# Three pairs of projection units of the second layer as seven half-size products each, with weight sums made by accumulating transfers

## The chip, the cores and the metric

The kernel runs on one core of a Trainium2 chip. Its time is the device time of one execution in microseconds (us); the kernel before takes 886.24 us, the median of three runs that lie between 886.05 and 886.3. The five engines are TensorE (PE, with its weight loads listed as PEld), VectorE (DVE), ScalarE (ACT), GpSimd (POOL) and SyncE (SP). Each works through its own list of instructions in order. SP issues nearly all loads; POOL issues a few.

## The reference

A trunk of two layers on 256 tokens of width 2048, all in float32. What matters here is the second layer's input projection `z = h @ w_in`:

```python
def odd_layer(x, norm, w_in, w_alpha, b_alpha, head_norm, v_norm, w_s, b_s, w_out):
    h = rms_norm(x, norm)
    z = h @ w_in                                  # (256, 2048) @ (2048, 6160)
    q, k, v, a_lr, gc, u, vd, gd = jnp.split(z, split_points(ODD_SIZES), axis=-1)
    log_a = jax.nn.log_sigmoid((a_lr @ w_alpha + b_alpha)) / GLA_TAU
    ...
    o = gla_chunked(heads(q, GLA_DK), heads(k, GLA_DK), heads(v, GLA_DV), heads(log_a, GLA_DK))
    yc = rms_norm(o, head_norm).reshape(bsz, seq, GLA_VW) * jax.nn.silu(gc)
    yd = spatial_gating(jax.nn.gelu(u), jax.nn.gelu(vd), w_s, b_s, v_norm) * jax.nn.silu(gd)
    return jnp.concatenate([yc, yd], axis=-1) @ w_out
```

The column widths are q 512, k 512, v 1024, a_lr 16, gc 1024, u 1024, vd 1024, gd 1024.

## The kernel before

Activations stand transposed in SBUF, 16 row blocks (k = 0 to 15) of 128, each with a high part and a low part of the 256 tokens: a float32 number is split into a value rounded to the type fp32r and the rest, so that a product of two float32 matrices is three fp32r products (high by high, high by low, low by high). `act2` is the tile that holds the second layer's activations so.

Weights come in **units**. A unit of 512 columns is four transfers of 1 MB, each a tile `raw` of 128 x 2048 that holds four row blocks. `halves` (L114) loads them through SP into a pool of three buffers and makes two half tiles of 128 x 1024 of each: ACT rounds it to `whi` (L123, "cast"), DVE subtracts to `wlo` (L73, "sub"). Both pools have four buffers, so casts run at most four half tiles ahead of the matmuls that read them. `by_token` (L135) then has `products` (L127) multiply: per row block and per token block b of 128 tokens three matmuls of 512 columns (L131 to L133). A half tile of a 512-column unit feeds 12 matmuls, a unit 96. The result is two PSUM banks, one per token block.

Smaller work (decays, attention-like parts, gates, transposes) is written as Python generators that are spawned after a unit and advanced by `tick` inside later units; a scheduler then fixes the order of each engine's list when the program is built, and picks buffers from the pools.

The second layer's units, by their first transfer in `w_in1`: a unit of 272 columns (v and a_lr, from `w_va`), 0 (256 columns of v), 2 (v), 6 (q), 10 (k), 14 and 18 (vd), 22 and 26 (gc), 30 and 34 (u), 38 and 42 (gd). `onward` (L492) ends the first layer: it transposes the residual and writes the last parts of `act2`.

Of the kernel before, what the change touches and what calls it, by code (L numbers as in the profile page):

```python
# [51 lines left out]
def trunk(ctx, tc, x, xt, lead, w_in0, w_out0, w_va, w_in1, w_out1, w_gate, small, dist, cst, w_alpha, w_s,  # L52
          r_balpha, r_hnorm, r_vnorm, r_fnorm, out):
    nc = tc.nc

    def pool(name, bufs, **kw):
        return ctx.enter_context(tc.tile_pool(name=name, bufs=bufs, **kw))

    one = pool("one", 1)
    actp = pool("actp", 2)  # L60
    rawp = pool("rawp", 3)
    hip = pool("hip", 4)
    lop = pool("lop", 4)
# [71 lines left out]
    def by_token(w, unit, act, n=512, order=None, before=None, during=None, ps=None):  # L135


        at = 0 if ps is None else LEAD
        ps = ps or [psm.tile([P, n], F32, name="ps", tag="ps") for _ in range(2)]
        order = order or list(range(KT))  # L140
        deep = 1024 // n if n != NVA else 4
        skip = at // (2 * deep)
        for hi, lo in halves(w, unit + skip, KT // (2 * deep) - skip, 2 * deep * n):
            if before is not None:
                for k in order[at:at + deep]:
                    before(k)
            for kk in range(deep):
                products(ps, act, order[at], hi[:, kk * n:(kk + 1) * n], lo[:, kk * n:(kk + 1) * n],
                         at == 0, at == KT - 1)
                if during is not None:  # L150
                    during(at, hi)
                at += 1
                tick(max(n // 256, 1))
        return ps

    def by_channel(w, unit, act):

        ps = [psm.tile([P, 2, T], F32, name="pc", tag="ps") for _ in range(2)]
        k = 0
        for hi, lo in halves(w, unit, 2):  # L160
            for kk in range(4):
                for c in range(2):
                    at = kk * 256 + c * P
                    wh, wl = hi[:, at:at + P], lo[:, at:at + P]
                    if k:
                        nc.tensor.matmul(ps[c][:, 1, :], wl, act[:, k, 0:T], start=False, stop=False)  # L166
                    nc.tensor.matmul(ps[c], wh, act[:, k, :], start=(k == 0), stop=(k == KT - 1))  # L167
                    if k == 0:
# [27 lines left out]
    sm = one.tile([P, S_ALL], F32, name="sm")  # L196
    cs = one.tile([P, C_ALL], F32, name="cs")
    xs = one.tile([P, 2, D], F32, name="xs")
    warm = one.tile([P, P], F32, name="warm")
    nc.vector.memset(warm, 0.0)  # L200
    table = tiny.tile([P, 1], F32, name="table", tag="table", bufs=1)
    nc.scalar.copy(table, warm[:, 0:1])
# [21 lines left out]
    for k in range(LEAD):  # L224
        raw = rawp.tile([P, T + 1024], F32, name="first", tag="raw")
# [4 lines left out]
        part = raw[:, 0:T]  # L230
# [294 lines left out]
    def decay(alr):  # L525
# [27 lines left out]
        for b in range(2):  # L553
# [13 lines left out]
            nc.scalar.activation(dec[:, :, 2 * b:2 * b + 2], dp[:, :, :, 0], AF.Exp)  # L567
            yield 3

    v1 = [big_tile([P, 2, 512], f"vv{c}") for c in range(2)]  # L570
    ps = by_token(w_va, 0, act2, n=NVA)
    alr = tiny.tile([P, 2, 16], F32, name="alr", tag="alr", bufs=1)
    for b in range(2):
# [8 lines left out]
        nc.scalar.activation(v1[1][:, b, :], ps[b], AF.Copy, scale=rs1[:, b:b + 1])  # L582
    drain()
    eb, enb, ebl = decays
    ps = by_token(w_in1, 6, act2)
    for b in range(2):
        nc.vector.scalar_tensor_tensor(out=eb[:, b, :], in0=ps[b], scalar=rs1q[:, b:b + 1], in1=eb[:, b, :],
                                       op0=ALU.mult, op1=ALU.mult)
    ps = by_token(w_in1, 10, act2)
    for b in range(2):  # L590
        for t in (enb, ebl):
            nc.vector.scalar_tensor_tensor(out=t[:, b, :], in0=ps[b], scalar=rs1[:, b:b + 1], in1=t[:, b, :],
                                           op0=ALU.mult, op1=ALU.mult)
    qt, kt, kd = eb, enb, ebl
    osb = []
# [61 lines left out]
        gla_ro.append(rsqrt_of(sso.rearrange("p a b -> p (a b)"), 8, T, "ro"))  # L657

    spawn(gla())


    wst = mid_tile([P, 4, P], "wst")
# [3 lines left out]
                            base=0, channel_multiplier=-1)  # L666
    vf = []
    mv = tiny.tile([P, 8, 2], F32, name="mv", tag="mv", bufs=1)
    for c in range(2):
        ps = by_token(w_in1, 14 + 4 * c, act2)  # L670
        t = big_tile([P, 2, 512], f"vf{c}")
        for b in range(2):
            nc.scalar.activation(t[:, b, :], ps[b], AF.Gelu_apprx_tanh, scale=rs1[:, b:b + 1])
            for i in range(2):
                bs = tiny.tile([P, 6], F32, name="bs", tag="bs", bufs=2)
                nc.vector.bn_stats(bs, t[:, b, i * T:(i + 1) * T])
                nc.vector.bn_aggr(mv[:, c * 4 + b * 2 + i, :], bs)
        vf.append(t)
# [5 lines left out]
    hn = big_tile([P, 2, 512], "hn")  # L684
    nc.gpsimd.dma_start(out=hn, in_=r_hnorm.partition_broadcast(P))

    yt1 = actp.tile([P, KT, 2 * T], F32R, name="yt1", tag="act")

    def transposed(src, k0, b):
        tp = psa.tile([P, 4, P], F32, name="tp", tag="a")  # L690
        for i in range(4):
            nc.tensor.transpose(tp[:, i, :], src[:, i * P:(i + 1) * P], ident)
        split(yt1, slice(k0, k0 + 4), b * P, P, tp)

    def gla_gate(c, ps):
        for b in range(2):
            sg = sp_tile([P, 512], "sgc")
            nc.scalar.activation(sg, ps[b], AF.Silu, scale=rs1[:, b:b + 1])
            nc.vector.tensor_mul(sg, sg, hn[:, c, :])
            for i in range(2):  # L700
                o = osb[b][:, c, i * T:(i + 1) * T]
                at = b * 4 + 2 * c + i
                nc.vector.scalar_tensor_tensor(out=o, in0=o, scalar=ro[:, at:at + 1], in1=sg[:, i * T:(i + 1) * T],
                                               op0=ALU.mult, op1=ALU.mult)
        for b in range(2):
            yield 4
            transposed(osb[b][:, c, :], 4 * c, b)

    def normed(c):
        for b in range(2):  # L710
            for i in range(2):
                t = vf[c][:, b, i * T:(i + 1) * T]
                at = c * 4 + b * 2 + i
                nc.vector.tensor_scalar(out=t, in0=t, scalar1=mv[:, at, 0:1], scalar2=rv[:, at:at + 1],
                                        op0=ALU.subtract, op1=ALU.mult)
            nc.vector.tensor_mul(vf[c][:, b, :], vf[c][:, b, :], vn[:, c, :])
            yield 6

    yd = []
# [189 lines left out]
```

## Time and profile before

| what | value |
|---|---|
| median of three runs | 886.24 us |
| the profiled execution | 885.52 us |
| its span | 883.4 us |
| PE busy | 873.2 us (99% of the span) |
| DVE busy | 530.6 us (60%) |
| ACT busy | 480.7 us (54%) |
| POOL busy | 13.2 us (1%) |
| DMA | 163.42 MB, mean 185 GB/s |
| granted TensorE clock | 0.998 |

The profiled execution took 885.52 us, of which 883.4 are the span from its first to its last recorded work; 2.1 us lie around it. It is 0.7 us under the median of the runs. A busy PE is not a PE at its peak, since matmuls overlap and their ends are modelled; the time of a stage is better read from the distance between starts. [...]

### The profile page before, as it was taken

How to read it: one execution, taken by the hardware profiler on the slowest of the kernel's cores; microseconds unless marked ns; L12 is line 12 of the kernel's file. 1: busy time of each engine (PE TensorE's matmuls, PEld its weight loads, DVE VectorE, ACT ScalarE, POOL GpSimd, SP SyncE). 2: the span in 40 equal slices, each digit the busy share in tenths (PEclk: the TensorE clock that was granted, in tenths of full speed). 3: DMA queues.
4: the chain of work that ended last, by engine and by line, in shares of the span. 5: the costliest groups of instructions: out<-in, count | busy, mean ns of one | idle time of the engine just before them, and what ended most of it. 6: DMA issues, size and time to landing. Idle time of an engine off the chain costs nothing.

```text
span 883.4 us, 11332 instructions
## 1 busy us (share of the span) xinstructions
PE 873.2 (99%) x4480; PEld 733.8 (83%) x4480; DVE 530.6 (60%) x770; ACT 480.7 (54%) x709; POOL 13.2 (1%) x27
## 2 busy tenths in 40 slices
PE   8999999999999999999999999999999999999996
PEld 7878888888888888888888988886688888888886
DVE  7596457667677576666555744564267554555562
ACT  5775556676676766554444564333555444544452
POOL 0100000000000000010000000000000000000000
PEclk9999999999999999999999999999999999999999
DMA  8875554454444435555455544552365544555532
GB/s 288 351 266 191 191 202 157 152 192 161 176 178 167 167 144 191 189 208 191 181 178 186 185 151 183 191 191 95 105 253 214 190 158 177 191 191 190 191 143 96
DMA packets 25492, 163.42 MB, mean 185 GB/s; under 512 B 2896, under 2 KB 3408, under 8 KB 7008
## 3 DMA queue, kind: packets, MB, share of 16 engines
q1 hardware_dynamic: 24048, 158.41, 49.9%
q0 software_dynamic: 1248, 4.23, 1.4%
q8 instruction: 35, 0.57, 0.3%
q14 instruction: 17, 0.14, 0.0%
q10 hardware_dynamic: 144, 0.07, 0.0%
HBM read 160.60 MB, written 2.10 MB: 184 GB/s over the span
## 4 chain that ended last, share of the span: by engine, by line
PE 94%; DVE 2%; DMA 1%; ACT 1%; issue 1%; POOL 0%; ACTq 0%
PE pc L167 20%; PE ps L131 18%; PE ps L132 18%; PE ps L133 18%; PE pc L166 10%; DVE wlo L73 1%; PE up L626 1%; DMA xs<-in_x 1%; PE pc L169 1%; PE sc L352 1%; PE gp L436 1%; PE gp L435 1%; ACT whi L123 1%; DVE act L212 0%; PE pt_ps L370 0%
## 5 line engine op out<-in xcount | busy, mean ns | idle before, releaser
L73 DVE TENSOR_TENSOR wlo<-raw,whi 128x1024 fp32r<-128x1024 f32 x280 | 341.7, 1223 | 259.0 <-ACT whi L123 258.8
L123 ACT CAST whi<-raw 128x1024 fp32r<-128x1024 f32 x280 | 293.7, 1052 | 306.2 <-PE ps L133 224.1
L167 PE MATMUL pc<-act,whi 128*128 128x512 f32 x768 | 269.7, 394 | 0.0
L131 PE MATMUL ps<-whi,act 128*128 128x512 f32 (+2 forms) x544 | 208.8, 386 | 0.8 <-DVE la_s L325 0.8
L166 PE MATMUL pc<-act,wlo 128*128 128x256 f32 x720 | 208.4, 289 | 0.0
L132 PE MATMUL ps<-wlo,act 128*128 128x512 f32 (+2 forms) x544 | 205.8, 379 | 1.0 <-DVE wlo L73 0.9
L133 PE MATMUL ps<-whi,act 128*128 128x512 f32 (+2 forms) x544 | 205.5, 378 | 0.0
L167 PEld LDWEIGHTS pc<-act,whi 128*128 128x128 f32 x768 | 142.6, 188 | 29.4
L166 PEld LDWEIGHTS pc<-act,wlo 128*128 128x128 f32 x720 | 135.8, 189 | 2.5 <-DVE wlo L73 0.8
L131 PEld LDWEIGHTS ps<-whi,act 128*128 128x128 f32 x544 | 102.1, 188 | 25.2 <-issue 6.5
L132 PEld LDWEIGHTS ps<-wlo,act 128*128 128x128 f32 x544 | 102.3, 188 | 20.2 <-DVE wlo L73 2.5
L133 PEld LDWEIGHTS ps<-whi,act 128*128 128x128 f32 x544 | 102.2, 188 | 19.0
L131 PE MATMUL ps<-whi,yt 128*128 128x512 f32 (+1 forms) x256 | 97.0, 379 | 0.0
L133 PE MATMUL ps<-whi,yt 128*128 128x512 f32 (+1 forms) x256 | 96.3, 376 | 0.0
L132 PE MATMUL ps<-wlo,yt 128*128 128x512 f32 (+1 forms) x256 | 96.2, 376 | 0.0
L133 PEld LDWEIGHTS ps<-whi,yt 128*128 128x128 f32 x256 | 48.2, 188 | 8.9
L132 PEld LDWEIGHTS ps<-wlo,yt 128*128 128x128 f32 x256 | 48.2, 188 | 8.6
L131 PEld LDWEIGHTS ps<-whi,yt 128*128 128x128 f32 x256 | 48.2, 188 | 8.4
L188 ACT ACTIVATE junk<-xs 128x512 f32<-128x512 f32 (+1 forms) x26 | 15.3, 591 | 15.7 <-DVE xs L771 14.3
L175 ACT COPY z<-pc 128x256 f32<-128x256 f32 x24 | 8.7, 372 | 13.0 <-PE pc L167 13.0
L175 ACT COPY qk<-pc 128x256 f32<-128x256 f32 x24 | 8.7, 372 | 12.1 <-PE pc L167 12.1
L428 DVE SCALAR_TENSOR_TENSOR xc<-z,sm,xc 128x255 f32<-128x255 f32 (+2 forms) x36 | 14.7, 475 | 0.0
(231 smaller groups left out, 621.5 us busy)
## 6 DMA issues: line engine op xcount, KB each, us to landing
raw<-in_w_in SPq DMA_DIRECT2D x108, 1024.0 KB, 4.8
raw<-in_w_out SPq DMA_DIRECT2D x32, 1024.0 KB, 4.8
raw<-in_w_va SPq DMA_DIRECT2D x2, 1088.0 KB, 5.0
xs<-in_x SPq DMA_DIRECT2D x2, 1024.0 KB, 6.0
out<-xs SPq DMA_DIRECT2D x8, 256.0 KB, 2.7
first<-in_lead SPq DMA_DIRECT2D x3, 640.0 KB, 6.1
xt<-in_xt SPq DMA_DIRECT2D x6, 256.0 KB, 7.5
wg<-in_w_gate POOLq DMA_DIRECT2D x6, 256.0 KB, 5.1
```

The lines of the kernel that those rows point to most:

```text
L73: nc.vector.tensor_tensor(out=o, in0=a, in1=hi.bitcast(F32), op=ALU.subtract)
L123: nc.scalar.copy(hi, raw[:, cols])
L131: nc.tensor.matmul(ps[b], xh, wh, start=first, stop=False)
L132: nc.tensor.matmul(ps[b], xh, wl, start=False, stop=False)
L133: nc.tensor.matmul(ps[b], xl, wh, start=False, stop=last)
L166: nc.tensor.matmul(ps[c][:, 1, :], wl, act[:, k, 0:T], start=False, stop=False)
L167: nc.tensor.matmul(ps[c], wh, act[:, k, :], start=(k == 0), stop=(k == KT - 1))
L169: nc.tensor.matmul(ps[c][:, 1, :], wl, act[:, k, 0:T], start=False, stop=False)
L175: nc.scalar.copy(dst, ps[:, 1, :])
L188: nc.scalar.activation(junk[:, :src.shape[-1]], src, AF.Square, accum_out=acc)
L352: nc.tensor.matmul(sc[:, 1:3, :], qk[:, 0, P:T], qk[:, 1, :], start=True, stop=True)
L428: nc.vector.scalar_tensor_tensor(out=xch[:, t:], in0=z[:, :T - t], scalar=cw[3 - t], in1=xch[:, t:], op0=ALU.mult, op1=ALU.add)
```

## The change

Two units that share the activations, A and B, are taken together as a pair. The activations are cut into four blocks (two halves of the 2048 rows by two token blocks), the weights into four (two halves of the rows by two units), and the 2 x 2 product is made by Strassen's scheme in Winograd's form: seven half-size products of 8 row blocks, one token block and 512 columns. One such product ("run") is 24 matmuls, a pair 168 instead of 192. Pairs are (6, 10), (14, 18) and (30, 34).

Three things are new. The **forms**, four sums of activation blocks, are made by DVE and split by ACT and DVE into a second tile `sums2` of the size of `act2`. The **weight sums** are made in place: a `raw` tile is loaded by SP, cast and multiplied, and then POOL issues a transfer that adds another 1 MB of weights onto what stands in it; one pair of tiles (x0) is loaded once and added to three times, another (y0) is added to once, a third (z0) only loaded. That is six plain transfers and eight adding ones of 1 MB in a pair, where two units had eight plain ones. The **combination** of the products takes two ACT copies and five DVE operations of 128 x 512. A half tile now feeds 6 matmuls, so that a pair has 28 casts and 28 subs where two units had 16 of each.

The pool of `raw` tiles grows from three to five buffers; `warm` and `rb` move into the pool of `sg`; the reserve that GpSimd's transfers use shrinks (`dynamic_dma_scratch_size=1024`). The gate units 22 and 26 move: 22 now stands between the first and the second pair, 26 between the second and the third, and their results wait in `sgc` tiles. `yt1` is made after the third pair.

```diff
-    rawp = pool("rawp", 3)
+    rawp = pool("rawp", 5)
...
+    def pair(w, ua, ub, act, forms):
+        f3, f5, f6, f7 = forms
+        x0, y0, z0 = ([rawp.tile([P, 2048], F32, name="raw", tag="raw") for _ in range(2)] for _ in range(3))
+        def load(raws, u):
+            for i, raw in enumerate(raws):
+                nc.sync.dma_start(out=raw, in_=w[u + i])
+        def add(raws, u):
+            for i, raw in enumerate(raws):
+                nc.gpsimd.dma_start(out=raw, in_=w[u + i], accum_op=ALU.add)
+        def run(ps, a, raws, first, last):
+            tile_, k0, b = a
+            for i, raw in enumerate(raws):
+                for s in range(2):
+                    cols = slice(s * 1024, (s + 1) * 1024)
+                    hi = hip.tile([P, 1024], F32R, name="whi", tag="whi")
+                    lo = lop.tile([P, 1024], F32R, name="wlo", tag="wlo")
+                    nc.scalar.copy(hi, raw[:, cols])
+                    sub(lo, raw[:, cols], hi)
+                    for kk in range(2):
...
+                        nc.tensor.matmul(ps, xh, wh, start=(first and j == 0), stop=False, skip_group_check=not first)
+                        nc.tensor.matmul(ps, xh, wl, start=False, stop=False, skip_group_check=not first)
+                        nc.tensor.matmul(ps, xl, wh, start=False, stop=(j == 7), skip_group_check=not first)
+                        tick(1)
...
+        load(x0, ua)
+        load(y0, ub + 2)
+        m12, m3, m56, m7 = bank(), bank(), bank(), bank()
+        run(m12, (act, 0, 0), x0, True, False)
+        s1 = mid_tile([P, 512], "s1")
+        nc.scalar.copy(s1, m12)
+        add(x0, ub)
+        run(m3, f3, y0, True, True)
+        add(y0, ub)
+        run(m56, f5, x0, True, False)
+        s5 = mid_tile([P, 512], "s5")
+        nc.scalar.copy(s5, m56)
+        add(x0, ub + 2)
+        run(m7, f7, y0, True, True)
+        load(z0, ua + 2)
+        run(m56, f6, x0, False, True)
+        add(x0, ua + 2)
...
+        run(m12, (act, 8, 0), z0, False, True)
+        m4 = bank()
+        run(m4, (act, 8, 1), x0, True, True)
+        nc.vector.tensor_tensor(out=s5, in0=m4, in1=s5, op=ALU.add)
+        return [m12, s5], [t, c22]
...
+    sums2 = actp.tile([P, KT, 2 * T], F32R, name="sums2", tag="act")
+    def make_forms():
+        for i in range(2):
...
+            s, r = (sp_tile([P, 4, P], n) for n in ("fs", "fr"))
+            minus(s, part(0, 1), part(8, 1))
+            minus(r, part(0, 1, T), part(8, 1, T))
+            plus(s, s, r)
+            keep(1, s)
+            yield 3
...
+    spawn(make_forms())
     ps = by_token(w_va, 0, act2, n=NVA)
...
-    ps = by_token(w_in1, 6, act2)
+    ps, ps_k = pair(w_in1, 6, 10, act2, forms2)
...
-    ps = by_token(w_in1, 10, act2)
...
+    keep_gate(0)
...
-    for c in range(2):
-        ps = by_token(w_in1, 14 + 4 * c, act2)
+    for c, ps in enumerate(pair(w_in1, 14, 18, act2, forms2)):
...
+    keep_gate(1)
...
-    for c in range(2):
-        ps = by_token(w_in1, 30 + 4 * c, act2)
+    for c, ps in enumerate(pair(w_in1, 30, 34, act2, forms2)):
...
-    nc = bacc.Bacc("TRN2", target_bir_lowering=False, num_devices=1)
+    nc = bacc.Bacc("TRN2", target_bir_lowering=False, num_devices=1, dynamic_dma_scratch_size=1024)
```

How the lists of instructions change is shown at three places. In their rows a name before the arrow is the tile written, names behind it the tiles read, numbers at a name tell buffers' tiles apart.

First POOL, from the last transfer of the first layer's end (`bal`) on. Before, it goes on with small transfers (`wst`, `vn`, `hn`) and a memset:

```order
L486 DMA bal_3682<-in_r_balpha 128x512
L663 DMA wst_5070<-in_w_s 128x512
L665 ISA
L665 AFFINE_SELECT wst_5070<-wst_5070 128x512
L603 MEMSET att_5096 128x1024
L683 DMA vn_5518<-in_r_vnorm 128x1024
L685 DMA hn_5520<-in_r_hnorm 128x1024
```

Now the eight adding transfers of the first pair stand there (4833 and 4834 are x0, 4835 and 4836 are y0):

```order
L555 DMA bal_3682<-in_r_balpha 128x512
L172 DMA raw_4833<-in_w_in1 128x2048
L712 MEMSET att_5176 128x1024
L172 DMA raw_4834<-in_w_in1 128x2048
L172 DMA raw_4835<-in_w_in1 128x2048
L172 DMA raw_4836<-in_w_in1 128x2048
L172 DMA raw_4833<-in_w_in1 128x2048
L172 DMA raw_4834<-in_w_in1 128x2048
L172 DMA raw_4833<-in_w_in1 128x2048
L172 DMA raw_4834<-in_w_in1 128x2048
L781 DMA wst_5362<-in_w_s 128x512
```

Each of the tiles x0 is named three times in that list, and each naming has to wait for the casts of the one before; the other two pairs have the same eight rows.

Second DVE, from the last sub of the 272-column unit to the second sub of unit 0. Before, little stands between them beside the last two parts of `act2`:

```order
L73 TENSOR_TENSOR wlo_4443<-raw_4412,whi_4442 128x1088
L507 TENSOR_TENSOR xg_4359<-tp_4354,sm_91 128x512
L73 TENSOR_TENSOR act2_3857<-xg_4359,act2_3857 128x4x128
L507 TENSOR_TENSOR xg_4380<-tp_4375,sm_91 128x512
L73 TENSOR_TENSOR act2_3857<-xg_4380,act2_3857 128x4x128
L73 TENSOR_TENSOR wlo_4480<-raw_4477,whi_4479 128x1024
L73 TENSOR_TENSOR wlo_4531<-raw_4477,whi_4530 128x1024
```

Now the operations on the forms (`fs`, `fr`, written by L649, and `sums2`) stand there:

```order
L73 TENSOR_TENSOR wlo_4514<-raw_4511,whi_4513 128x1024
...
L73 TENSOR_TENSOR sums2_4332<-fs_4335,sums2_4332 128x4x128
L73 TENSOR_TENSOR act2_3857<-xg_4367,act2_3857 128x4x128
L649 TENSOR_TENSOR fr_4336<-fr_4336,act2_3857 128x512
L73 TENSOR_TENSOR act2_3857<-xg_4392,act2_3857 128x4x128
L649 TENSOR_TENSOR fs_4335<-act2_3857,fr_4336 128x512
L73 TENSOR_TENSOR sums2_4332<-fr_4336,sums2_4332 128x4x128
L649 TENSOR_TENSOR fs_4335<-fs_4335,act2_3857 128x512
...
L73 TENSOR_TENSOR sums2_4332<-fs_4465,sums2_4332 128x4x128
L73 TENSOR_TENSOR wlo_4569<-raw_4511,whi_4568 128x1024
```

Of the 28 form operations 20 stand between the last sub of the 272-column unit and the second sub of unit 0 (`wlo_4569`), and 26 ahead of its third (`wlo_4606`).

Third SP, behind the loads of the 272-column unit. Before, one run of plain loads; now the six loads of each pair (L168) stand between the loads of the other units (L118):

```order
L118 DMA raw<-in_w_in 128x2048 x46
```

```order
L118 DMA raw<-in_w_in 128x2048 x6
L168 DMA raw<-in_w_in 128x2048 x6
L118 DMA raw<-in_w_in 128x2048 x4
L168 DMA raw<-in_w_in 128x2048 x6
L118 DMA raw<-in_w_in 128x2048 x4
L168 DMA raw<-in_w_in 128x2048 x6
L118 DMA raw<-in_w_in 128x2048 x8
```

SP issues 40 instead of 46 loads there; the 24 adding transfers are POOL's.

## Rows read from the trace of the kernel before

**Rows 1.** The page: busy time by engine, and the chain of waits

```profile
PE 873.2 (99%) x4480; PEld 733.8 (83%) x4480; DVE 530.6 (60%) x770; ACT 480.7 (54%) x709; POOL 13.2 (1%) x27
...
PE 94%; DVE 2%; DMA 1%; ACT 1%; issue 1%; POOL 0%; ACTq 0%
```

**Rows 2.** Windows: stretch and length, busy us by engine, clock, DMA share, GB/s

```profile
487.00:500.00 13.00, 13.00 (x107) 13.00 (x106) 9.38 (x15) 8.11 (x13) 0.00 (x0) 1.00 0.54 190
500.00:514.00 14.00, 14.00 (x104) 12.54 (x103) 8.54 (x9) 10.30 (x12) 0.00 (x0) 1.00 0.40 138
...
538.80:560.60 21.80, 21.80 (x98) 18.06 (x97) 9.84 (x9) 9.65 (x10) 0.00 (x0) 1.00 0.48 170
560.60:582.40 21.80, 21.80 (x98) 18.06 (x97) 11.16 (x11) 8.44 (x8) 0.00 (x0) 1.00 0.53 189
```

**Rows 3.** Timeline of DVE in unit 6: start, duration, instruction, idle before

```profile
545.97 1.23 DVE L73 TENSOR_TENSOR wlo<-raw,whi 128x1024 fp32r<-128x1024 f32 x1 [1.50 <-ACT whi L123]
548.68 1.23 DVE L73 TENSOR_TENSOR wlo<-raw,whi 128x1024 fp32r<-128x1024 f32 x1 [1.49 <-ACT whi L123]
```

**Rows 4.** Waits of SP's queue in units 6 and 10: total, times, longest

```profile
SPq L118 <- DVE wlo L73: 41.4, 8, 7.0
```

**Rows 5.** Timeline of DVE from the first layer's end into unit 0

```profile
465.49 1.23 DVE L73 TENSOR_TENSOR wlo<-raw,whi 128x1024 fp32r<-128x1024 f32 x1 [0.30 <-ACT whi L123]
466.63 0.68 DVE L507 TENSOR_TENSOR xg<-tp,sm 128x512 f32<-128x512 f32 x1
...
488.25 1.29 DVE L73 TENSOR_TENSOR wlo<-raw,whi 128x1088 fp32r<-128x1088 f32 x1 [0.23 <-ACT whi L123]
489.46 0.68 DVE L507 TENSOR_TENSOR xg<-tp,sm 128x512 f32<-128x512 f32 x1
490.06 0.15 DVE L192 TENSOR_REDUCE sum<-ssq 128x2 f32<-128x8 f32 x1
...
498.13 1.23 DVE L73 TENSOR_TENSOR wlo<-raw,whi 128x1024 fp32r<-128x1024 f32 x1 [1.76 <-ACT whi L123]
499.64 0.60 DVE L574 TENSOR_SCALAR alr<-ps,rs 128x16 f32<-128x16 f32 x2 [0.28 <-PE ps L133]
```

**Rows 6.** Groups of DVE instructions by shape, 470 to 560 us: busy us, mean ns

```profile
L538 DVE TENSOR_TENSOR la<-lp,bal 128x512 f32<-128x512 f32 x2 | 1.4, 690 | 1.0 <-PE lp L537 1.0
L540 DVE SCALAR_TENSOR_TENSOR eb<-la 128x1024 f32<-128x1024 f32 x1 | 1.2, 1224 | 0.0
```

**Rows 7.** The page: the cast, the costliest group of ACT

```profile
L123 ACT CAST whi<-raw 128x1024 fp32r<-128x1024 f32 x280 | 293.7, 1052 | 306.2 <-PE ps L133 224.1
```

**Rows 8.** DMA from 20 to 30 us, the densest stretch of plain loads

```profile
DMA packets 927, 4.01 MB, mean 401 GB/s; under 512 B 109, under 2 KB 109, under 8 KB 548
...
q1 hardware_dynamic: 925, 3.99, 98.0%
```

**Rows 9.** The page: transfers by issuer, count, size, us to landing

```profile
raw<-in_w_in SPq DMA_DIRECT2D x108, 1024.0 KB, 4.8
...
wg<-in_w_gate POOLq DMA_DIRECT2D x6, 256.0 KB, 5.1
```

**Rows 10.** The tile wg: POOL's issues (ns min/median/max) and their landing

```profile
L416 POOL DMA_DIRECT2D wg<-in_w_gate x6: 536/536/683, 110.1 to 252.4; - x6
...
DMA to landing us min/median/max: 3.2/5.1/5.7
```

**Rows 11.** DMA in units 6 and 10, 538.8 to 582.4 us

```profile
DMA packets 1083, 7.83 MB, mean 180 GB/s; under 512 B 128, under 2 KB 128, under 8 KB 128
...
q1 hardware_dynamic: 1080, 7.80, 50.1%
```

More of the change, by code (lines that the diff above doesn't have):

```diff
@@ L154, in by_token, with bank @@
         return ps
+    def pair(w, ua, ub, act, forms):
[17 more added lines that the diff above has]
+                    for kk in range(2):
+                        j = 4 * i + 2 * s + kk
+                        wh, wl = hi[:, kk * 512:(kk + 1) * 512], lo[:, kk * 512:(kk + 1) * 512]
+                        xh = tile_[:, k0 + j, b * P:(b + 1) * P]
+                        xl = tile_[:, k0 + j, T + b * P:T + (b + 1) * P]
+                        nc.tensor.matmul(ps, xh, wh, start=(first and j == 0), stop=False, skip_group_check=not first)
+                        nc.tensor.matmul(ps, xh, wl, start=False, stop=False, skip_group_check=not first)
+                        nc.tensor.matmul(ps, xl, wh, start=False, stop=(j == 7), skip_group_check=not first)
+                        tick(1)
+        def bank():
+            return psm.tile([P, 512], F32, name="ps", tag="ps")
+        load(x0, ua)
[15 more added lines that the diff above has]
+        add(x0, ua + 2)
+        t = mid_tile([P, 512], "t")
+        nc.vector.tensor_tensor(out=t, in0=m56, in1=s1, op=ALU.subtract)
+        c22 = s1
+        nc.vector.tensor_tensor(out=c22, in0=m7, in1=t, op=ALU.add)
+        nc.vector.tensor_tensor(out=t, in0=m3, in1=t, op=ALU.add)
+        nc.vector.tensor_tensor(out=s5, in0=s5, in1=c22, op=ALU.subtract)
+        run(m12, (act, 8, 0), z0, False, True)
[3 more added lines that the diff above has]
+        return [m12, s5], [t, c22]
@@ L198, in trunk @@
     xs = one.tile([P, 2, D], F32, name="xs")
-    warm = one.tile([P, P], F32, name="warm")
+    warm = sp.tile([P, P], F32, name="warm", tag="sg", bufs=3)
     nc.vector.memset(warm, 0.0)
@@ L271, in trunk @@
     keep_v(1)
-    rb = one.tile([P, T], F32, name="rb")
+    rb = sp.tile([P, T], F32, name="rb", tag="sg", bufs=3)
     act1 = actp.tile([P, KT, 2 * T], F32R, name="act1", tag="act")
@@ L568, in decay, with part, plus, minus @@
             yield 3
+    sums2 = actp.tile([P, KT, 2 * T], F32R, name="sums2", tag="act")
+    forms2 = [(sums2, k0, b) for k0, b in ((0, 0), (8, 0), (8, 1), (0, 1))]
+    def make_forms():
+        for i in range(2):
+            def part(k0, b, lo=0):
+                return act2[:, k0 + 4 * i:k0 + 4 * i + 4, lo + b * P:lo + (b + 1) * P].bitcast(F32)
+            def plus(o, a, b, op=ALU.add):
+                nc.vector.tensor_tensor(out=o, in0=a, in1=b, op=op)
+            def minus(o, a, b):
+                plus(o, a, b, ALU.subtract)
+            def keep(f, src):
+                _, k0, b = forms2[f]
+                split(sums2, slice(k0 + 4 * i, k0 + 4 * i + 4), b * P, P, src)
+            s, r = (sp_tile([P, 4, P], n) for n in ("fs", "fr"))
[4 more added lines that the diff above has]
+            yield 3
+            minus(r, part(0, 0), s)
+            plus(r, r, part(0, 0, T))
+            keep(2, r)
+            yield 3
+            minus(s, part(8, 0), r)
+            plus(s, s, part(8, 0, T))
+            keep(0, s)
+            yield 3
+            s, r = (sp_tile([P, 4, P], n) for n in ("fs", "fr"))
+            minus(s, part(0, 1), part(0, 0))
+            minus(r, part(0, 1, T), part(0, 0, T))
+            plus(s, s, r)
+            keep(3, s)
+            yield 3
     v1 = [big_tile([P, 2, 512], f"vv{c}") for c in range(2)]
+    spawn(make_forms())
     ps = by_token(w_va, 0, act2, n=NVA)
@@ L588, in trunk @@
                                        op0=ALU.mult, op1=ALU.mult)
-    ps = by_token(w_in1, 10, act2)
     for b in range(2):
         for t in (enb, ebl):
-            nc.vector.scalar_tensor_tensor(out=t[:, b, :], in0=ps[b], scalar=rs1[:, b:b + 1], in1=t[:, b, :],
+            nc.vector.scalar_tensor_tensor(out=t[:, b, :], in0=ps_k[b], scalar=rs1[:, b:b + 1], in1=t[:, b, :],
                                            op0=ALU.mult, op1=ALU.mult)
@@ L659, in trunk, with keep_gate @@
     spawn(gla())
+    gates = [None, None]
+    def keep_gate(c):
+        ps = by_token(w_in1, 22 + 4 * c, act2)
+        gates[c] = big_tile([P, 2, 512], f"sgc{c}")
+        for b in range(2):
+            nc.scalar.activation(gates[c][:, b, :], ps[b], AF.Silu, scale=rs1[:, b:b + 1])
+    keep_gate(0)
     wst = mid_tile([P, 4, P], "wst")
@@ L685, in trunk @@
     nc.gpsimd.dma_start(out=hn, in_=r_hnorm.partition_broadcast(P))
-    yt1 = actp.tile([P, KT, 2 * T], F32R, name="yt1", tag="act")
     def transposed(src, k0, b):
@@ L693, in transposed, with gla_gate @@
         split(yt1, slice(k0, k0 + 4), b * P, P, tp)
-    def gla_gate(c, ps):
+    def gla_gate(c):
         for b in range(2):
-            sg = sp_tile([P, 512], "sgc")
-            nc.scalar.activation(sg, ps[b], AF.Silu, scale=rs1[:, b:b + 1])
+            sg = gates[c][:, b, :]
             nc.vector.tensor_mul(sg, sg, hn[:, c, :])
@@ L704, in gla_gate, with gla_out @@
                                                op0=ALU.mult, op1=ALU.mult)
-        for b in range(2):
             yield 4
-            transposed(osb[b][:, c, :], 4 * c, b)
+    def gla_out():
+        for c in range(2):
+            for b in range(2):
+                yield 4
+                transposed(osb[b][:, c, :], 4 * c, b)
     def normed(c):
@@ L719, in trunk @@
     yd = []
-    for c in range(2):
-        ps = by_token(w_in1, 22 + 4 * c, act2)
-        spawn(gla_gate(c, ps))
-        spawn(normed(c))
+    spawn(gla_gate(0))
+    spawn(normed(0))
+    keep_gate(1)
+    spawn(gla_gate(1))
+    spawn(normed(1))
     def mix(c, t):
@@ L735, in mix @@
             yield 2
-    for c in range(2):
-        ps = by_token(w_in1, 30 + 4 * c, act2)
+    for c, ps in enumerate(pair(w_in1, 30, 34, act2, forms2)):
         t = big_tile([P, 2, 512], f"yd{c}")
@@ L743, in trunk @@
         spawn(mix(c, t))
+    yt1 = actp.tile([P, KT, 2 * T], F32R, name="yt1", tag="act")
+    spawn(gla_out())
     def sgu_gate(c, ps):
```

## The prediction

> **What bounds the kernel now.** I read the page first. Its busy line and its chain of waits [rows 1] show one engine: PE is busy 873.2 of 883.4 us and holds 94% of the chain that ended last. A busy PE need not be a full one, so I went on to the stages that change. In the windows of units 6 and 10 [rows 2] PE is busy in every microsecond at clock 1.00, DVE 21.0 and ACT 18.1 of 43.6 us. The timeline of DVE there [rows 3] gives the pace: subs start 2.71 us apart, each half tile feeds 12 matmuls, so a matmul takes 0.227 us, and DVE idles 1.5 us before each sub, because ACT's cast waits until PE frees a buffer. SP's loads wait the same way, for DVE to release a tile [rows 4], and the transfers fill half of the DMA engines' time [rows 11]. So before, each part waits for PE, and PE for nothing. Fewer matmuls save time only as long as casts, subs and transfers still keep up with twice the work for each matmul.
>
> **What is removed.** 192 - 168 = 24 matmuls in a pair, 72 in all, at 0.227 us: -16.3 us. A pair falls from 43.6 us (the two units of [rows 2]) to 168 x 0.227 = 38.1 us at best.
>
> **Casts and subs.** 28 of each in a pair. ACT: 28 x 1.05 = 29.4 us [rows 7]. DVE: one sub to the next start is 466.63 - 465.49 = 1.14 us [rows 5], 28 x 1.14 = 31.9, and five combinations at 0.6 make 34.9. Both fit under 38.1, DVE with 3 us to spare. But a half tile now covers only 1.36 us of PE where it covered 2.72, and the operations that empty a pair's banks stand in DVE's and ACT's lists just ahead of the next subs and casts. Four to six of them of 0.6 to 0.7 us are 2.4 to 4.2 us against two covered half tiles, 2.7 us: I take 1.3 us a pair, 4 us in all (bounds 0 and 12, the whole of them uncovered).
>
> **The forms.** 28 DVE operations of 128 x 512. One takes 0.69 us alone [rows 6], and from one start to the next 490.06 - 489.46 = 0.60 [rows 5]: 16.8 us, in a stretch where DVE had 27.0 - 17.9 = 9.1 us free (487 to 514 us, [rows 2]). The order puts 26 of them ahead of unit 0's third sub. From 489.46 on stand 26 x 0.6 = 15.6, four operations for act2 (2.4), two subs (2.3), the decays' work (2 x 0.6 and 1.1) and six small ones (1.2): that sub starts at 513.3 and ends at 514.5. PE wants it near 507: unit 0 begins when the 272-column unit ends, at about 499.6 by the operation on alr [rows 5], two half tiles take 5.4 and small PE work 2. So PE waits about 7 us. Bounds: 0, if the order's slack covers it, and 16.8, if nothing does; I take 7.
>
> **The weight sums.** Here the trace of before shows no such operation. A plain MB occupies the 16 DMA engines for 1.0486/401 = 2.61 us, at 98% busy [rows 8]. POOL's own transfers of 256 KB cost 0.54 us of issue and land after 3.2 to 5.7 us [rows 10], against 4.8 us for SP's whole MB [rows 9]. An adding transfer brings in the new MB and must also bring in the old one, since the sum needs both, and writes one. From below it costs as much as a plain one (f = 1, 2.61 us); nothing excludes that if the two intakes overlap. From above, a fetch, a fetch and a store done one after the other as three plain transfers (f = 3, 7.8 us); below nothing is excluded, because bytes are added, none removed. The rows nearest to it are those of the dense stretch, where one intake already fills the engines. I take f = 2, 5.2 us, and keep 1 and 3.
>
> [...]
>
> Now the chain in a pair. x0's tiles go cast, add, cast, add, cast, add, cast, and each add waits for DVE's last sub of its tile. Casts run four half tiles ahead, so x0's last half is cast when PE starts the pair: cast 1.05, sub 1.23, issue 0.54, and 2.8 us into the pair the second add begins; the first is nearly through. From there seven adds and four plain MB (z0's second tile and three loads of the next unit, which share the same 16 engines) stand in the queue, with the next add always ready before the last has landed if f is 2. Behind the last add: a cast 1.05, two subs 2.4, six matmuls 1.4, together 4.8. A pair therefore takes 7.6 + (7f + 4) x 2.61 us, or 38.1 if that is less. For f = 2: 7.6 + 47.0 = 54.6, that is 11.0 more than 43.6; three pairs: +33. The removed matmuls are inside this number; PE waits 16.5 us in each pair, in front of the casts of x0 and y0.
>
> Who else waits: behind the adds on POOL stand the memset of att, wst, vn and hn. att's memset comes after the first add alone, and the others are wanted a unit later, so I cost them at nothing. On SP the next unit's loads stand behind z0's second load, which waits for y0's release. Its first cast then waits for one landing, which is in the four plain MB above. The moved gate units 22 and 26 keep their work and give the DMA queue some 21.8 us each, in which four plain MB need 10.4: the queue is empty again before the next pair. The smaller POOL reserve, `warm` and `rb` cost nothing: no instruction is added, and each row of these adds is one of 8 KB as in a plain load.
>
> **The sum.** +33 (pairs, with -16.3 inside) + 7 (forms) + 4 (ends of pairs) = +44 us on the profiled execution's 885.5 (883.4 of span and 2.1 around it): 929.5. The median of the runs is 0.7 above that execution: 930 us.
>
> **Rivals.**
> - *An adding MB costs little more than a plain one (f up to 1.3).* For it: nothing in the trace says that the engines' intake and not their output is the limit, and half their time is free [rows 11]. Against it: the dense stretch is full with one intake. Then a pair at f = 1 takes 38.1 (the chain alone 36.3), -16.5 in all, + 7 + 4 = -5.5: 880 us, faster. It turns where three pairs save less than 11, at 39.9 us a pair, f = 1.20; f = 1.3 would give 891.
> - *It costs three plain ones.* [...] 7.6 + 25 x 2.61 = 72.8 a pair, 3 x 29.2 + 11 = +99: 984 us.
> - *The transfers are hidden and DVE is late instead.* For it: DVE's 34.9 of 38.1 us leave 3 us a pair, and the order puts the state updates of gla and its row sums into the second pair; against it: they are small. Each microsecond of them beyond 3 adds one. With 5 us too many in one of the three pairs the first rival's 880 becomes 885, no gain. This is the side of the first rival that holds its 0.04 of no change.
>
> **How the numbers follow.** About what can be told from no change is 0.2%, 1.8 us. The forecast, with f from 1.3 to 2.5, has 0.58; its own range is 891 to 957 (f = 2.5: 63.7 a pair, +71). The first rival has 0.28, of which 0.04 lie within 0.2%; the second 0.14. Faster 0.24, the same 0.04, slower 0.72. The range of 8 in 10 takes in the first rival at f = 1 with some of the forms hidden, 876, and ends at f = 2.7, 968; beyond it is most of the second rival.
>
> **What would show it.** In the profile after, PE has 24 matmuls fewer in each pair and idles before the matmuls of runs 3 to 5 and 7, released by sub or cast, and these by an adding transfer on POOL's queue. The three pairs last about 55 us each where 38 are possible; the DMA share in them is near 1 at about 300 GB/s or under. POOL's landing times lie above 7 us. About 7 us of PE's idle time stand in unit 0, released by the subs behind the forms. I am wrong if the adds land in 5 us and the pairs last 38 to 40 us (first rival), if PE waits in front of runs on the forms and not on weights, or if idle time between runs brings PEclk under 1.00, which I have costed at nothing.

## The result and the profile after

The changed kernel takes 928.59 us, the median of four runs between 927.18 and 929.95, against 886.2 us before: the ratio is 1.048, with an interval of 1.046 to 1.050. The profiled execution took 927.18 us, its span 925.5. 930 us were forecast, with 891 to 957 as the forecast's own range. Kernel times are medians of fast runs, so that one slow run, 928.09 us of the first version with sums in device memory, is left out of its median.

The page of the changed kernel first: busy time, GpSimd's queue (packets, MB, share of 16 engines), the chain of waits, the group of the pairs' casts, and the issues of the second layer's weights.

```profile
PE 879.9 (95%) x4408; PEld 730.0 (79%) x4408; DVE 594.0 (64%) x849; ACT 521.2 (56%) x759; POOL 33.2 (4%) x51
...
q0 software_dynamic: 4704, 29.40, 15.3%
...
PE 80%; DMA 9%; DVE 5%; issue 3%; ACT 3%; POOL 0%; ACTq 0%; POOLq 0%; DVEq 0%
...
L181 ACT CAST whi<-raw 128x1024 fp32r<-128x1024 f32 x84 | 85.3, 1048 | 83.0 <-DMA raw<-in_w_in 46.5
...
raw<-in_w_in SPq DMA_DIRECT2D x102, 1024.0 KB, 4.9
raw<-in_w_in POOLq DMA_DIRECT2D x24, 1024.0 KB, 9.7
```

Against [rows 1] PE's part of the chain has fallen to 80%, and transfers of raw hold 9% of it. ACT's casts in the pairs waited 46.5 us for transfers, and an adding MB lands after 9.7 us, twice the 4.9 of a plain one from SP. PE is busier by 6.7 us with 72 matmuls fewer: a busy PE is not a full one, and in the pairs its granted clock was 0.88, 0.94 and 0.91, as the next view shows. That view has the stretch, its length, busy time of PE, PEld, DVE, ACT and POOL, the granted clock (PEclk, 1.00 is full speed), the DMA share and GB/s. The first three stretches are those of the forms and unit 0, the others the three pairs, each from its first to its last matmul.

```profile
487.00:500.00 13.00, 13.00 (x103) 12.80 (x103) 12.77 (x23) 9.21 (x15) 0.00 (x0) 1.00 0.40 150
500.00:514.00 14.00, 12.06 (x67) 9.45 (x65) 14.00 (x24) 6.37 (x11) 0.00 (x0) 0.88 0.23 75
514.00:524.00 10.00, 7.55 (x54) 7.04 (x55) 7.56 (x8) 9.37 (x11) 0.00 (x0) 1.00 0.30 107
547.50:603.20 55.70, 45.74 (x169) 34.66 (x168) 33.68 (x32) 29.88 (x32) 7.29 (x9) 0.88 0.96 244
635.90:696.00 60.10, 53.67 (x225) 37.06 (x224) 34.76 (x39) 37.19 (x56) 7.08 (x9) 0.94 0.86 208
721.80:778.10 56.30, 46.98 (x177) 34.92 (x175) 35.34 (x37) 30.45 (x34) 7.09 (x9) 0.91 0.96 238
```

The pairs last 55.7, 60.1 and 56.3 us. In the first and third the engines are 96% full and move only 244 and 238 GB/s, where plain loads moved 401 at 98% [rows 8]. The second pair has 56 matmuls of gla in it. What PE waits for most from 487 to 780 us (total, times, longest):

```profile
PE ps L188 <- ACT whi L181: 18.4, 7, 5.2
PE ps L189 <- DVE wlo L73: 7.2, 12, 0.8
```

PE waits for casts and subs of the pairs, and these for transfers, as the chain through the first pair shows (start, duration, what):

```profile
553.63 1.06 ACT whi L181
554.72 1.24 DVE wlo L73
...
556.66 0.84 POOL raw L172
...
559.43 24.50 DMA raw<-in_w_in x2
584.03 1.05 ACT whi L181
585.11 1.24 DVE wlo L73
586.39 0.79 PE ps L189
```

A cast, its sub and POOL's issue release two transfers that take 24.5 us in a row, and only then the next cast of this chain and the matmuls behind it go on. The adds' own line on POOL (ns min/median/max, first and last start; who waited for them; the time to landing):

```profile
L172 POOL DMA_DIRECT2D raw<-in_w_in x24: 842/858/897, 543.9 to 763.2; - x24
...
  ACT whi L181: 46.5, 12
...
DMA to landing us min/median/max: 7.8/9.7/18.2
```

The last add of the first pair and the cast behind it (timelines of POOL and ACT, and this add's time from issue to landing):

```profile
587.87 0.87 POOL L172 DMA_DIRECT2D raw<-in_w_in  x1 [6.62 <-DVE wlo L73]
...
DMA to landing us min/median/max: 10.1/10.1/10.1
...
598.03 2.00 ACT L181 CAST whi<-raw 128x1024 fp32r<-128x1024 f32 x2 [3.02 <-PE ps L190]
```

The add landed at 597.9 us, and the cast began 0.1 us later; PE released the cast's buffer in the same tenth.

In unit 0 DVE's list ran without a break up to the third sub:

```profile
513.12 0.69 DVE L649 TENSOR_TENSOR fr<-act 128x512 f32<-128x512 f32 x1
513.72 1.22 DVE L73 TENSOR_TENSOR wlo<-raw,whi 128x1024 fp32r<-128x1024 f32 x1
```

It started at 513.72 us, where 513.3 was worked out. (In the listing of DVE's new order ahead of the forecast, the first row, `wlo_4514`, is unit 0's first sub and not the last of the 272-column unit; the counts of 20 and 26 operations there hold.)

### The profile page after: what moved, and what is told of

Its sections match the earlier page's. It is cut to its first block, busy times and chain, and to the rows that moved or that the text cites. A ratio compares the mean times of both kernels' runs of the same rounds, so it can differ in the third digit from the quotient of the medians.

```text
span 925.5 us, 11413 instructions
## 1 busy us (share of the span) xinstructions
PE 879.9 (95%) x4408; PEld 730.0 (79%) x4408; DVE 594.0 (64%) x849; ACT 521.2 (56%) x759; POOL 33.2 (4%) x51
## 3 DMA queue, kind: packets, MB, share of 16 engines
q0 software_dynamic: 4704, 29.40, 15.3%
## 4 chain that ended last, share of the span: by engine, by line
PE 80%; DMA 9%; DVE 5%; issue 3%; ACT 3%; POOL 0%; ACTq 0%; POOLq 0%; DVEq 0%
PE pc L236 19%; PE ps L132 13%; PE ps L133 13%; PE ps L131 13%; PE pc L235 9%; DMA raw<-in_w_in 8%; DVE wlo L73 3%; PE ps L188 1%; PE ps L189 1%; PE ps L190 1%; ACT whi L181 1%; PE pc L238 1%; PE up L735 1%; PE sc L421 1%; PE gp L505 1%
## 5 line engine op out<-in xcount | busy, mean ns | idle before, releaser
L73 DVE TENSOR_TENSOR wlo<-raw,whi 128x1024 fp32r<-128x1024 f32 x316 | 382.6, 1224 | 241.9 <-ACT whi L123 168.9
L123 ACT CAST whi<-raw 128x1024 fp32r<-128x1024 f32 (+1 forms) x232 | 242.7, 1052 | 221.0 <-PE ps L133 138.7
L132 PE MATMUL ps<-wlo,act 128*128 128x512 f32 (+2 forms) x352 | 132.7, 378 | 5.6 <-DVE wlo L73 5.6
L131 PE MATMUL ps<-whi,act 128*128 128x512 f32 (+2 forms) x352 | 132.2, 382 | 2.8 <-ACT whi L123 2.1
L181 ACT CAST whi<-raw 128x1024 fp32r<-128x1024 f32 x84 | 85.3, 1048 | 83.0 <-DMA raw<-in_w_in 46.5
L133 PE MATMUL ps<-whi,act 128*128 128x512 f32 (+2 forms) x352 | 132.0, 376 | 0.0
L132 PEld LDWEIGHTS ps<-wlo,act 128*128 128x128 f32 x352 | 67.5, 192 | 19.1 <-DVE wlo L73 7.3
L131 PEld LDWEIGHTS ps<-whi,act 128*128 128x128 f32 x352 | 66.8, 191 | 16.5 <-ACT whi L123 2.9
L133 PEld LDWEIGHTS ps<-whi,act 128*128 128x128 f32 x352 | 67.4, 192 | 11.6
L188 PE MATMUL ps<-whi,sums 128*128 128x512 f32 x96 | 43.2, 450 | 18.4 <-ACT whi L181 18.4
L189 PE MATMUL ps<-wlo,sums 128*128 128x512 f32 x96 | 43.4, 452 | 5.3 <-DVE wlo L73 5.2
L188 PEld LDWEIGHTS ps<-whi,sums 128*128 128x128 f32 x96 | 20.5, 214 | 26.8 <-ACT whi L181 21.6
```

Of the source, the lines that this page charges most:

```text
L123: nc.scalar.copy(hi, raw[:, cols])
L131: nc.tensor.matmul(ps[b], xh, wh, start=first, stop=False)
L132: nc.tensor.matmul(ps[b], xh, wl, start=False, stop=False)
L133: nc.tensor.matmul(ps[b], xl, wh, start=False, stop=last)
L181: nc.scalar.copy(hi, raw[:, cols])
L188: nc.tensor.matmul(ps, xh, wh, start=(first and j == 0), stop=False, skip_group_check=not first)
```

## The experiments

The theory is that of the forecast: an adding MB costs two plain ones of engine time, the adds set the length of a pair, and the forms cost some 7 us in unit 0. All ratios are against the kernel before on the same chip.

**Adds as plain loads.** The line that issues an add loses its adding.

```
-                nc.gpsimd.dma_start(out=raw, in_=w[u + i], accum_op=ALU.add)
+                nc.gpsimd.dma_start(out=raw, in_=w[u + i])
```

> The 24 adding transfers of the pairs become plain loads of the same 1 MB into the same tiles, from the same queue, at the same places in the order; the adding itself is left out. Theory (an adding MB costs two plain ones, 5.2 us, and the chain of adds sets a pair): by 7.6 + (7f + 4) x 2.61 with f = 1 a pair falls from 55-60 us to about 38-40, the clock stays at 1.00, and the time is 875-885 us, under the kernel before. Rival (casts, subs and the GpSimd issue pace a pair, whatever the transfer does): a pair stays over 50 us, the time over 915 us.

Measured: 882.82 us, ratio 0.9971 (0.9952 to 0.9989), 45.8 us under the changed kernel with the same instructions on every engine. Its page and its windows of the three pairs:

```profile
q0 software_dynamic: 4704, 29.40, 9.0%
...
raw<-in_w_in POOLq DMA_DIRECT2D x24, 1024.0 KB, 5.7
```

```profile
546.00:585.20 39.20, 38.63 (x169) 31.37 (x168) 33.51 (x32) 30.13 (x32) 6.94 (x9) 1.00 0.87 330
617.50:668.30 50.80, 50.80 (x225) 36.10 (x225) 34.82 (x40) 38.84 (x58) 4.76 (x9) 1.00 0.66 250
692.80:732.90 40.10, 39.67 (x177) 32.34 (x175) 35.33 (x37) 31.32 (x35) 4.76 (x9) 1.00 0.87 336
```

The pairs take 39.2, 50.8 and 40.1 us at clock 1.00, so casts, subs and POOL's issues can hold the pace; the adding alone set it. The price comes out of two rows: the GpSimd queue, with the same packets and bytes, fills 15.3% of 925.5 us with adding (141.6 us) and 9.0% of 879.7 without (79.2). That is 62.4 / 24 = 2.60 us more for each MB. On the plain 2.61 of the dense stretch this makes f = 2.0. On this queue a plain MB is a little dearer: the kernel before has the queue's other transfers alone,

```profile
q0 software_dynamic: 1248, 4.23, 1.4%
```

which is 12.4 us of 883.4, so that a plain MB takes (79.2 - 12.4) / 24 = 2.78 us, an adding one 5.38, and f is 1.9.

**Half of each add.** Only 1024 of the 2048 columns are added.

```
-                nc.gpsimd.dma_start(out=raw, in_=w[u + i], accum_op=ALU.add)
+                nc.gpsimd.dma_start(out=raw[:, 0:1024], in_=w[u + i][:, 0:1024], accum_op=ALU.add)
```

> Each adding transfer adds only the first 1024 of its 2048 columns, so half of the weight sums is left out; count, order and issue of the adds stay. Theory (what an add costs is engine time in proportion to its bytes): half an add is 2.6 us, as much as a plain MB; a pair is 38-40 us and the time 875-890 us. Rival (an add costs a fixed latency for each step of the chain, a round of wait, issue and landing): seven waits stay nearly as they are, a pair falls by under a quarter, the time is over 910 us.

Measured: 882.55 us, ratio 0.9958 (0.9940 to 0.9977), as with plain loads. Its page, and its window of the first pair:

```profile
q0 software_dynamic: 4704, 16.81, 9.7%
...
raw<-in_w_in POOLq DMA_DIRECT2D x24, 512.0 KB, 6.9
```

```profile
547.00:585.70 38.70, 38.44 (x170) 31.45 (x170) 33.91 (x32) 30.57 (x32) 7.22 (x9) 1.00 0.91 237
```

The number of adds, their order and their waits are those of the changed kernel, POOL's issue takes as long (0.856 us in the median), and the first pair takes 38.7 us. So it is not the round of wait, issue and landing that costs, but the engines' time for the bytes: half the bytes with adding fill about what all of them fill without (9.7 against 9.0%).

**No forms.** Plain blocks of act2 stand in their place.

```
-    sums2 = actp.tile([P, KT, 2 * T], F32R, name="sums2", tag="act")
-    forms2 = [(sums2, k0, b) for k0, b in ((0, 0), (8, 0), (8, 1), (0, 1))]
+    forms2 = [(act2, k0, b) for k0, b in ((0, 0), (8, 0), (8, 1), (0, 1))]
...
-    spawn(make_forms())
```

> The four activation forms are not computed (plain blocks of act2 stand in their place); the pairs and their adds stay. Theory (PE waits in unit 0 behind the 28 DVE operations, 4.4 us of gaps and 3.4 us at half the clock): 6 to 8 us less, 920-923 us. Rival (DVE has room for them, the wait in unit 0 is from elsewhere): within 1.5 us of the changed kernel, 927-930 us.

Measured: 917.58 us, ratio 1.0355 (1.0338 to 1.0373): 11.0 us under the changed kernel, more than the 6 to 8 expected. Unit 0's windows there:

```profile
500.00:514.00 14.00, 14.00 (x103) 12.46 (x102) 8.66 (x9) 10.30 (x13) 0.00 (x0) 1.00 0.38 136
514.00:524.00 10.00, 10.00 (x45) 8.22 (x44) 4.87 (x4) 6.91 (x10) 0.00 (x0) 1.00 0.52 175
```

PE is busy throughout at clock 1.00, where it idled 1.9 and 2.5 us in the changed kernel and ran at 0.88 in the first of the two. The two profiled executions lie 7.7 us apart (927.18 and 919.45), less than the medians: the one is the fastest of its four runs, the other the slowest. The rival (DVE has room, the wait is from elsewhere) is out.

**One pair alone.** Units 14, 18, 30 and 34 go back to `by_token`, in the new order.

```
-    for c, ps in enumerate(pair(w_in1, 14, 18, act2, forms2)):
+    for c in range(2):
+        ps = by_token(w_in1, 14 + 4 * c, act2)
...
-    for c, ps in enumerate(pair(w_in1, 30, 34, act2, forms2)):
+    for c in range(2):
+        ps = by_token(w_in1, 30 + 4 * c, act2)
```

> Only the first pair (units 6 and 10) is done as seven products; the other four units are done as in the kernel before, in the new order. Theory (each pair loses 12 us or a little more against two plain units, and the forms 7): 886 + 7 + 12 = 903-907 us. Rival 1 (a cost that falls once, at the first pair or in the forms): 925-930 us. Rival 2 (the first pair is nearly free and the later ones lose, since gla and the gates lie in them): 890-895 us.

Measured: 906.36 us, ratio 1.0224 (1.0208 to 1.0239), 20.5 over the kernel before, inside what the theory gave. Its windows, the pair and the rest of the second layer's units that follow:

```profile
547.00:603.80 56.80, 46.71 (x169) 34.55 (x169) 34.10 (x32) 29.94 (x32) 7.36 (x9) 0.88 0.98 248
603.80:780.00 176.20, 175.34 (x786) 136.12 (x786) 98.05 (x129) 82.22 (x104) 2.17 (x4) 1.00 0.51 182
```

The pair takes 13.2 us more than the two units of [rows 2], and behind it PE is as full as before. The remaining 22.2 us of the changed kernel come with the other two pairs, 11 each on the mean: the cost does not fall once, and the later pairs do not bear it alone.

**The forms spread.** All is computed; the four steps are further apart.

```
-            yield 3
+            yield 7
...
```

> All of the changed kernel is computed; only the steps of the forms are 7 ticks apart where they were 3, so that the 28 operations are spread over DVE's spare time up to the end of unit 2. Theory (the forms cost only because they stand in one block ahead of unit 0's third sub): the time falls as without the forms, to 917-921 us, and PE no longer waits in unit 0. Rival (16.8 us of DVE work find no room in this stretch, however they are placed): 924 us or more.

Measured: 921.23 us, ratio 1.0391 (1.0375 to 1.0407), 7.4 under the changed kernel, just over what the theory gave and clearly under the rival's 924. Unit 0's windows:

```profile
500.00:514.00 14.00, 13.96 (x102) 12.29 (x101) 12.43 (x19) 10.61 (x14) 0.00 (x0) 1.00 0.35 132
514.00:524.00 10.00, 10.00 (x46) 8.21 (x45) 10.00 (x13) 8.27 (x12) 0.00 (x0) 1.00 0.51 174
```

PE's waits in unit 0 are gone with all 28 operations still there. It was their place that cost, not their sum.

**Sums made ahead in device memory.** The 24 sums of 1 MB are written to device memory while layer 0 runs; the pairs load 14 plain MB each through SP. The core of the edit, on top of the spread forms (`ahead` is called once per half tile of `halves`):

```
+    def ahead(hi):
+        pace[0] += 1
+        if not later or not pace[1] or pace[0] % pace[1]:
+            return
+        o, a, more = later.pop(0)
+        nc.gpsimd.dma_start(out=o[0:1, 0:8], in_=hi[0:1, 0:8].bitcast(F32))
+        nc.gpsimd.dma_start(out=o, in_=a)
+        nc.gpsimd.dma_start(out=o, in_=more, accum_op=ALU.add)
...
-        add(x0, ub)
-        run(m3, f3, y0, True, True)
-        add(y0, ub)
-        run(m56, f5, x0, True, False)
+        run(m3, f3, plain(ub + 2), True, True)
+        run(m56, f5, summed(0), True, False)
...
```

> As e5, and the weight sums (24 of 1 MB for the three pairs) are made ahead of time in device memory, from the start of layer 0's 24 channel units on, by 24 plain copies and 24 adding transfers from one place in device memory to another, one of each about every 15 us; the pairs then load 14 plain MB each through SyncE's queue. Theory (an adding MB costs two plain ones of the 16 engines, and half of their time is free before the pairs): 24 x (2.6 + 5.2) = 188 us of engine time fit into some 430 us where about half, 215, is free; pairs of 38-40 us (some 50 with gla's work inside), no fall of the clock, 868-876 us, faster than both kernels. Rival (the extra transfers delay the loads of layer 0, so that PE waits there): the pairs are short all the same, but the channel units lose over 10 us together, 883 us or more.

Measured: 918.23 us, ratio 1.0354 (1.0334 to 1.0374). The time is on the rival's side, its reason only in part. The pairs first, then the longest waits of ACT and of PE from 95 to 540 us:

```profile
590.50:628.80 38.30, 38.30 (x170) 31.52 (x170) 33.87 (x32) 31.01 (x32) 0.00 (x0) 1.00 0.85 331
661.00:711.90 50.90, 50.90 (x225) 36.16 (x225) 34.89 (x40) 39.06 (x58) 1.10 (x2) 1.00 0.72 266
736.30:775.50 39.20, 39.20 (x175) 32.19 (x174) 36.16 (x39) 32.60 (x36) 0.53 (x1) 1.00 0.94 357
```

```profile
ACT whi L148 <- DMA ws<-whi: 107.8, 17, 11.9
...
PE gp L523 <- DMA wg<-in_w_gate: 8.0, 2, 4.2
```

The pairs are full: 38.3, 50.9 and 39.2 us. What was lost lies ahead of them: ACT's casts waited 107.8 us for the small transfer that paces each sum. It reads a cast half tile, so that buffer stays taken until it has landed, and it stands on GpSimd's queue behind the adds. That is ACT's waiting; PE idled 30.8 us from 95 to 590 us, 8.8 of them for the loads of wg, which stand on the same queue behind the same adds and landed 13.1 us after their issue in the median, against 5.1 [rows 9], and its clock was 0.96 there. Both waits are for transfers that stand behind adds on that queue. Whether the engines' time has a part in them, the next run tests.

**The same without that wait.** DVE copies eight columns, the small transfer reads the copy, a sum begins every six half tiles, and wg is loaded through ScalarE's queue.

```
-        nc.gpsimd.dma_start(out=o[0:1, 0:8], in_=hi[0:1, 0:8].bitcast(F32))
+        at = tiny.tile([P, 8], F32, name="at", tag="at")
+        nc.vector.tensor_copy(at, hi[:, 0:8].bitcast(F32))
+        nc.gpsimd.dma_start(out=o[0:1, 0:8], in_=at[0:1, :])
...
-                nc.gpsimd.dma_start(out=wg, in_=w_gate[2 * q + n])
+                nc.scalar.dma_start(out=wg, in_=w_gate[2 * q + n])
...
-    pace[1] = 5
+    pace[1] = 6
```

> As e6, with what held layer 0 there taken away: the small transfer that paces each sum reads a copy made by DVE (24 tiny DVE operations) and no longer a cast half tile, so ACT's buffers are free at once; a sum is begun every 6 half tiles, not 5; and the six loads of wg go through ScalarE's queue, not behind the sums on GpSimd's. Theory (e6 lost its time to these waits, 108 us of ACT's casts behind the pacing transfer, and not to the engines' time): layer 0 ends where it does without the sums, and the pairs of 38, 51 and 39 us measured in e6 give 868-876 us, faster than both kernels. Rival (the 188 us of extra engine time themselves delay the loads, since the engines are near 0.9 full there): channel units still wait for whi and wlo behind SyncE's loads, 885 us or more.

Measured: 872.93 us, ratio 0.9851 (0.9834 to 0.9867): 12.5 us faster than the kernel before and 55.7 faster than the changed one. Its windows of the sums' stretch and of the pairs:

```profile
95.00:540.00 445.00, 444.93 (x2488) 385.56 (x2488) 300.11 (x480) 269.76 (x427) 44.75 (x71) 1.00 0.88 283
539.30:581.40 42.10, 39.79 (x169) 31.06 (x168) 34.14 (x32) 30.53 (x32) 3.53 (x5) 1.00 0.98 369
613.70:664.60 50.90, 50.90 (x226) 36.20 (x226) 34.93 (x40) 39.05 (x58) 1.11 (x2) 1.00 0.72 268
688.90:728.20 39.30, 39.30 (x175) 32.24 (x175) 36.20 (x39) 32.70 (x36) 0.53 (x1) 1.00 0.94 359
```

The engines are 88% full from 95 to 540 us, and PE loses 0.07 us there. So the engines' time alone does not cost what the first version lost. The pacing, its rate and the queue of wg were changed together, and what each was worth is not shown. The adds are about as dear as before:

```profile
q0 software_dynamic: 8448, 52.99, 23.2%
```

This is 203 us of 873.4, where 24 plain MB at 2.78 and 24 adding ones at 5.38 give an estimate of 196, and small transfers stand on the queue beside them. The adds only stand where nobody waits for them. The first pair begins before the last sums have landed and takes 42.1 us, 3 to 4 more than it could.

## Why the prediction was right, point by point

Its chain was the right one. Its sum, +44 us, met +42.4 with errors of both signs, and that it came within 2 us is in part luck. The last row of the table is what the others leave of +42.4, and no run measured it by itself.

| term | forecast | measured | from |
|---|---|---|---|
| 72 matmuls removed | -16.3 | -12.5, with what is left of the last row | sums ahead, forms spread |
| adds, over a pair of 38.1 us | 3 x 16.5 = 49.5 | 45.8 | adds as plain loads |
| forms | +7 | 7.4 to 11.0, of it 7.0 to 7.2 ahead of the pairs | forms spread, no forms |
| ends of pairs | +4 | 1.9 to 5.5, the rest of +42.4 | 42.4 + 16.3 - 45.8 - forms |

*The price of an add.* f = 2 was chosen between 1 and 3; the rows of the queue give 1.9 to 2.0. That a second intake fills the engines was the author's estimate: the runs show 2.60 us more for each adding MB, and none tells a second read from another cost of the same size.

*The length of a pair.* 7.6 + (7f + 4) x 2.61 gave 54.6; the first and third took 55.7 and 56.3. The path in it holds too: in the first pair the last add landed 50.4 us behind the pair's first matmul, where 2.8 + 47.0 = 49.8 was worked out, in the third 51.2, and in all three pairs the cast behind it began 0.1 us later. The second took 60.1, but 50.8 with plain adds, so adding cost it 9.3 us: PE was busy for 53.7 of the 60.1 us there, since gla's matmuls filled a part of the waits. The forecast took the three pairs for alike and so mis-sized the term: 16.5 + 9.3 + 16.2 = 42.0 us inside the pairs, and 3.8 outside them. By the starts and ends of the windows 0.4 and 1.3 of these lie between the pairs and 0.6 behind the last; 1.5 lie ahead of the first pair, and the two traces are that far apart already at the first matmul of the 272-column unit (487.95 against 486.40 us), ahead of every add, so these are not the adds'.

*The forms.* The third sub came 0.4 us from its forecast time. PE idled 4.4 us in unit 0 where 7 had been forecast, and the clock fell to 0.88 behind that wait, which was not in the working. The clock's part is an estimate from that row: 14 x 0.12 = 1.7 us. What the stretch lost in all has the forecast size: from the first matmul of the 272-column unit to the first of the first pair PE took 59.6 us (487.95 to 547.51 us), without the forms 52.3 (486.56 to 538.88) and with them spread 52.5 (486.50 to 539.04), 7.0 to 7.2 us less. That the size was met with a shorter wait and a clock that nobody had reckoned with is luck. The two runs agree up to the first pair; the 3.6 us between their times, and what the 11.0 has more than 7.2, lie behind that point or between one execution and the next. The second pair, 60.1 us in the changed kernel, took 63.8 without the forms and 65.0 with them spread. Why it is longer there stays open.

*The ends of the pairs and DVE.* With sums that come in time a pair takes 38.3 to 39.3 us against 38.1 worked out, with DVE busy for 33.9 to 36.2 of it. The third rival, DVE late, is out, and 1.3 us a pair was an upper figure.

*The first rival.* Its mechanism was wrong, its arithmetic good: at f = 1 it gave 880 us, and plain loads in the adds' place took 882.8.

*What was costed at nothing.* Of what would speak against the forecast, one thing came: the clock fell in the pairs, to 0.88, 0.94 and 0.91. It did not break the sum, since PE was not what set a pair there: the cast behind the last add began 0.1 us after the landing in each pair, so PE's low clock can have lengthened a pair only by delaying an earlier sub and with it an add. The two pairs without gla are 1.1 and 1.7 us over the formula. What of this is the clock's was not measured, as no run kept PE busy in the waits.

## What to carry to other kernels

Add up the DMA engines' time for every transfer that a stage needs, an adding one at its measured price (1.9 to 2.0 plain ones here), and set it against the stage's time on the engine that is to be relieved: here 7 adds and 4 loads are 47 us against 38. The saving on the bound engine was paid for with a resource that was half idle (50.1% full in units 6 and 10 before [rows 11]), and it was a saving only once the payment was made at another time: moved ahead of the pairs, as many adds left 12.5 of the 16.3 us of removed matmuls as a gain. Work that is new on an engine with spare time wants to be spread over that time (spread, the forms took 7.4 us less), and a small transfer that paces others should read a buffer that nobody needs back (the casts waited 107.8 us for one that read theirs).

## What the runs showed of the hardware that was not expected

TensorE's granted clock fell behind some of PE's waits. In windows of 2 us of the changed kernel's first pair, with the columns as above:

```profile
564.00:566.00 2.00, 0.37 (x2) 0.00 (x0) 0.00 (x0) 0.47 (x1) 0.26 (x1) 1.00 1.06 221
566.00:568.00 2.00, 0.71 (x2) 0.30 (x2) 1.39 (x2) 1.53 (x2) 0.58 (x1) 0.72 1.08 225
568.00:570.00 2.00, 2.00 (x5) 1.63 (x6) 0.97 (x1) 0.00 (x0) 0.00 (x0) 0.50 0.99 205
570.00:572.00 2.00, 2.00 (x6) 1.54 (x6) 0.53 (x1) 1.61 (x3) 0.00 (x0) 0.50 0.98 205
...
574.00:576.00 2.00, 2.00 (x10) 1.39 (x8) 0.13 (x1) 0.00 (x0) 0.00 (x0) 1.00 0.98 283
```

PE stood nearly idle from 564 to 568 us; then the granted clock was 0.50, and 5 or 6 matmuls of 512 columns fitted into 2 us where the windows at 1.00 count 10 or 11. So slow matmuls stood behind this wait, in which PE shows as fully busy (2.00 of 2 us). In unit 0 more was lost than the length of the wait: PE idled 4.4 us, the clock was 0.88 from 500 to 514 us, and the stretch up to the first pair was 7.0 to 7.2 us longer than in the two runs without that wait.

The issue of an adding MB takes POOL 0.858 us, of a plain one of the same shape 0.527 in the run with plain loads; the wg loads were 0.54 [rows 10]. And a transfer of a few bytes on GpSimd's queue landed behind the adds ahead of it: in the first version with sums in device memory 23 of the 24 pacing transfers were issued behind an add, each landed 0.2 to 4.0 us after that add, and all 24 took this long (us min/median/max):

```profile
DMA to landing us min/median/max: 1.7/10.3/15.3
```
